# Sums of squares of MLA's queries taken while the queries arrive, and one root for all tokens; MLA's key roots for two token tiles at a time

## The chip, the cores and the metric

The kernel runs on one core of a Trainium2 chip. The time is that of one execution on the device, in microseconds (us). The engines are TensorE (PE; its weight loads are PEld), VectorE (DVE), ScalarE (ACT), GpSimd (POOL) and SyncE (SP), which only issues DMAs here.

## What is computed

One layer of a decoder for 1024 prompt tokens and 32 sample tokens (8 sequences of 4): a SwiGLU block, a mixer with two groups of heads side by side (a gated delta rule, GDN, and multi-head latent attention, MLA), and a second SwiGLU block. The change lies in the mixer's input, where one projection gives GDN's and MLA's raw values. MLA's part of the reference, cut to the norms that matter:

```python
def rms_norm(x, g):
    y = x * lax.rsqrt(jnp.mean(x * x, axis=-1, keepdims=True) + NORM_EPS)
    return y * g
...
    q = q_raw.reshape(B, T, 8, 64 + 32)                  # 8 heads of 96 columns
    qn = rms_norm(q[..., :64], qn_g)
    qr = apply_rope(rms_norm(q[..., 64:], qr_g), cos, sin)
    c = rms_norm(ckv_raw, ckv_g)                          # 128 wide
...
    kn = rms_norm(jnp.einsum('tr,rhd->thd', c, w_uk), kn_g)   # 8 heads of 64
```

So each token has 16 roots for its queries (per head one over 64 columns and one over 32) and 8 for its keys.

## The kernel before

All 1056 tokens go through together, as four blocks of 264 for the projections and as nine tiles for token-wise work: eight of 128 prompt tokens, and one (index 8) of the 32 sample tokens. Products of fp32 values are made from three matmuls of high and low halves (`mm3`, lines 127 to 129).

`mixer_in` is the stage of the change. Its order of work is the string `ORDER = "k0 k1 m0 m1 k2 k3 c0 I0 m2 m3 q0 m4 m5 z0 F0 q1 z1 q2 v0 q3 z2 v1 v2 v3 z3"`. Letters with weights (k, q, v, z for GDN, m for MLA's queries, c for its latent) are projections of 128 columns: `proj` loads the weights, splits them into halves `whi` (ScalarE) and `wlo` (GpSimd, four pieces, line 101; the first two sets on VectorE), multiplies the four token blocks (24 matmuls into a bank `pp` each), and after each block calls `hook`, which moves every generator in `self.active` on to its next `yield`. The first three sets (`bakr`, which holds the gates and the rotary key, then k0 and k1) go together, block by block. What follows a projection is such a generator:

- `mla_q_post` (m0 to m5): the 128 query columns are turned to tokens by TensorE (`to_tokens`, bank `ptk`, line 725), up to four tiles a bank; `sink` copies them to `mqt` (ScalarE, L1167), and two DMAs store them in DRAM (`qr_d`).
- `mla_q_finish` (F0, once all six are done, one tile after the other): a DMA loads the 768 columns of one tile (`mq`); a square (`mqs`, ScalarE, L1183), two reductions (VectorE, L1186), two scalings (L1187) and a root `hs` of ten VectorE instructions (`rsqrt`: L731, then three Newton steps of L737, L738, L739) follow; then the multiplications by the root (L1191, VectorE), by the gain (GpSimd, four pieces) and the rotation (`rope`, `rp`, VectorE and GpSimd by turns), and a DMA stores `qc_d`.
- `mla_c_post` (c0): the latent, its norm and transposed halves `cTh` and `cTl`, the rotary key, and then for each tile the key product `pkn`, its square `knq` (ScalarE, L1247), sum `kns` (VectorE, L1251), root `knr` (`pow_rs`, L760, and `rsqrt`), the value product `pv` and its copy `vtok` (ScalarE), and `kcat`, the scaled keys (VectorE L1263, GpSimd pieces, a GpSimd copy), stored in `kc_d`; values go to `v_d`.
- GDN's k, q and v: a convolution `cy` of four taps (ScalarE, then VectorE L938 three times), a SiLU back into `raw` (L940, L941), `to_tokens`, a sum of squares by the same scheme (`tsq` L954, one buffer; `tss` L955; root `trs`), the scaled `tok` (L963), transposes back (`pch`, L978) and products of pairs (`pk`, `dml`). `invert` (I0) solves triangular systems on VectorE (`inv`, `M`, lines 1107 and 1109).

Most tiles of the stage are the ten equal slots of tag `r` in the pool `tw`; PSUM has four banks of tag A (projections) and four of tag B (all else). `pieces(n, ...)` is n GpSimd instructions. The previous stage's last normalised input `nt` is read by `halve` (L372, L373).

The order on each engine is found by the framework's planner when the program is built: it plays the program through with a cost model of its own and gives each engine what is ready, first by the written order. GpSimd is exempt in this stage (`MW = ("Pool",)`): it keeps the written order, and its queue is strictly in turn. A tile that takes the place of an older one waits until that one is released.

Of the kernel before, what the change touches and what calls it, by code (L numbers as in the profile page):

```python
# [31 lines left out]
H = 8  # L32
# [52 lines left out]
class Kernel:  # L85
# [1075 lines left out]
    def mla_q_post(self, m, row, tp, ps):  # L1161
        nc = self.nc
        yield
        tok = self.r(tp, [P, NTL, P], "mqt")

        def sink(t0, n, sz, pt):
            nc.scalar.copy(tok[:sz, t0:t0 + n, :], pt[:sz, 0:n, :])  # L1167
        self.to_tokens(row, P, ps, sink)
        nc.sync.dma_start(out=self.qr_d[0:8, :, m * P:(m + 1) * P].rearrange("t p c -> p t c"), in_=tok[:, 0:8])
        nc.sync.dma_start(out=self.qr_d[8, :NS, m * P:(m + 1) * P], in_=tok[:NS, 8])  # L1170
        self.done["m"] += 1

    def mla_q_finish(self, t, rp, tp):

        nc = self.nc
        sz = P if t < 8 else NS
        q = self.r(rp, [P, 1, H, 96], "mq")
        if sz < P:
            nc.vector.memset(q, 0.0)
        qf = q.rearrange("p t h d -> p (t h d)")  # L1180
        nc.sync.dma_start(out=qf[:sz], in_=self.qr_d[t, :sz])
        sq = self.r(rp, [P, H, 96], "mqs")
        nc.scalar.activation(sq, q[:, 0], AF.Square)  # L1183
        ss = tp.tile([P, 3, 2, H], F32, tag="hs2", name="hs2", bufs=2)
        for n, (d0, d1) in enumerate(((0, 64), (64, 96))):
            nc.vector.tensor_reduce(out=ss[:, 0, n], in_=sq[:, :, d0:d1], axis=AX.X, op=ALU.add)  # L1186
            nc.vector.tensor_scalar(ss[:, 0, n], ss[:, 0, n], 1.0 / (d1 - d0), EPS, ALU.mult, ALU.add)  # L1187
        yield
        self.rsqrt(*(ss[:, n].rearrange("p a h -> p (a h)") for n in (1, 0, 2)))
        for n, (d0, d1) in enumerate(((0, 64), (64, 96))):  # L1190
            nc.vector.tensor_tensor(out=q[:, 0, :, d0:d1], in0=q[:, 0, :, d0:d1], in1=ss[:, 1, n].unsqueeze(2).to_broadcast([P, H, d1 - d0]), op=ALU.mult)  # L1191
        self.pieces(4, q[:, 0], q[:, 0], self.g_q.unsqueeze(1).to_broadcast([P, H, 96]), ALU.mult)
        yield
        self.rope(q[:, :, :, 64:96], H, q[:, :, :, 64:96], tp, t)
        if sz == P:
            nc.sync.dma_start(out=self.qc_d[t], in_=qf)
        else:
            nc.gpsimd.tensor_copy(self.qs, q[:NS, 0])
        yield
# [6 lines left out]
    def mla_c_post(self, row, tp, mp, ps, rp):  # L1206
        nc, o = self.nc, self.o
        yield
        c = self.r(rp, [P, NTL, 1, P], "ctok")
        nc.vector.memset(c[:, 8], 0.0)  # L1210

        def sink(t0, n, sz, pt):
            nc.scalar.copy(c[:sz, t0:t0 + n, 0, :], pt[:sz, 0:n, :])
        self.to_tokens(row, P, ps, sink)
        yield
        self.head_norm(c, 1, P, self.g_ckv, tp)
        yield
        nc.sync.dma_start(out=o["new_ckv_prompt"][0, 0].rearrange("(t p) c -> p t c", p=P), in_=c[:, 0:8, 0, :])
        nc.sync.dma_start(out=o["new_ckv_sample"][0].rearrange("s q c -> (s q) c"), in_=c[:NS, 8, 0, :])
        nc.gpsimd.tensor_copy(self.cs, c[:NS, 8, 0, :])  # L1220
        yield
        self.cTh, self.cTl = (self.r(rp, [P, NT], nm, F32R) for nm in ("cTh", "cTl"))
        for t0, n, sz in ((0, 4, P), (4, 4, P), (8, 1, NS)):
            pt = ps.tile([P, 512], F32, tag="B", name="pct")
            for t in range(n):
                nc.tensor.transpose(pt[:, t * P:t * P + sz], c[:sz, t0 + t, 0, :], self.ident[:sz, :sz])
            w = (n - 1) * P + sz
            nc.scalar.copy(self.cTh[:, t0 * P:t0 * P + w], pt[:, :w])
            nc.vector.tensor_tensor(out=self.cTl[:, t0 * P:t0 * P + w], in0=pt[:, :w], in1=f(self.cTh[:, t0 * P:t0 * P + w]), op=ALU.subtract)
            if t0 == 8:  # L1230
                nc.scalar.copy(self.csT, pt[:, :NS])
        yield
        kr = self.tb[:, :, 16:48].unsqueeze(2)
        self.head_norm(kr, 1, 32, self.g_kr, tp)
        self.kr = mp.tile([P, NTL, 1, 32], F32, name="kr")
        self.rope(kr, 1, self.kr, tp)
        nc.sync.dma_start(out=o["new_krope_prompt"][0, 0].rearrange("(t p) c -> p t c", p=P), in_=self.kr[:, 0:8, 0, :])
        nc.sync.dma_start(out=o["new_krope_sample"][0].rearrange("s q c -> (s q) c"), in_=self.kr[:NS, 8, 0, :])
        nc.gpsimd.tensor_copy(self.krs, self.kr[:NS, 8, 0, :])
        yield  # L1240
        for t in range(NTL):
            yield
            sz = P if t < 8 else NS
            pk = ps.tile([P, 512], F32, tag="B", name="pkn")
            self.mm3(pk[:sz], self.cTh[:, t * P:t * P + sz], self.cTl[:, t * P:t * P + sz], self.wuk[0], self.wuk[1], True, True)
            sq = tp.tile([P, 512], F32, tag="knq", name="knq", bufs=1)
            nc.scalar.activation(sq[:sz], pk[:sz], AF.Square)  # L1247
            ss = tp.tile([P, H], F32, tag="kns", name="kns", bufs=2)
            if sz < P:
                nc.vector.memset(ss, 1.0)  # L1250
            nc.vector.tensor_reduce(out=ss[:sz], in_=sq[:sz].rearrange("p (h d) -> p h d", h=H), axis=AX.X, op=ALU.add)  # L1251
            rs = tp.tile([P, H], F32, tag="knr", name="knr", bufs=2)
            self.pow_rs(rs, ss, H, 1.0 / 64, tp)
            if sz < P:
                nc.gpsimd.tensor_copy(self.rsn, rs[:NS])
                continue
            pv = ps.tile([P, 512], F32, tag="B", name="pv")
            self.mm3(pv, self.cTh[:, t * P:t * P + sz], self.cTl[:, t * P:t * P + sz], self.wuv[0], self.wuv[1], True, True)
            v = tp.tile([P, 512], F32, tag="vtok", name="vtok", bufs=1)
            nc.scalar.copy(v, pv)  # L1260
            nc.sync.dma_start(out=self.v_d[t], in_=v)
            kc = self.r(rp, [P, H, 96], "kcat")
            nc.vector.tensor_tensor(out=kc[:, :, 0:64], in0=pk.rearrange("p (h d) -> p h d", h=H), in1=rs.unsqueeze(2).to_broadcast([P, H, 64]), op=ALU.mult)  # L1263
            self.pieces(2, kc[:, :, 0:64], kc[:, :, 0:64], self.g_kn.unsqueeze(1).to_broadcast([P, H, 64]), ALU.mult)
            nc.gpsimd.tensor_copy(kc[:, :, 64:96], self.kr[:, t, :, :].to_broadcast([P, H, 32]))
            nc.sync.dma_start(out=self.kc_d[t], in_=kc.rearrange("p h d -> p (h d)"))

    def proj_z(self, m, tp, ps):
        nc = self.nc
# [14 lines left out]
    def mixer_in(self):  # L1284
# [12 lines left out]
        with tc.tile_pool(reuse_waits="tile", name="pswa", bufs=4, space=PSUM) as pa, tc.tile_pool(reuse_waits="tile", name="pswb", bufs=4, space=PSUM) as pb, tc.tile_pool(reuse_waits="tile", name="mw", bufs=1) as mp, tc.tile_pool(reuse_waits="tile", name="tw", bufs=1) as tp:  # L1297
            ps = Banks(A=pa, B=pb)

            def start(t, ml):  # L1300
                m = int(t[1])
                if t[0] == "k":
                    self.conv(4 + m, tp, ps, lambda raw: self.gdn_k(m, raw, tp, ps))
                elif t[0] == "q":
                    self.conv(m, tp, ps, lambda raw: self.gdn_q(m, raw, tp, ps))
                elif t[0] == "v":
                    self.conv(8 + m, tp, ps, lambda raw: self.gdn_v(m, raw, tp, ps))
                elif t[0] == "c":
                    self.mla_c(ml, mp, ps, tp)
                elif t[0] == "m":  # L1310
                    self.mla_q(m, tp, ps)
                elif t[0] == "z":
                    self.proj_z(m, tp, ps)
                elif t[0] == "I":
                    self.active.append(self.once("k", 4, self.invert(ml, tp)))
                elif t[0] == "F":
                    self.active.append(self.once("m", 6, self.in_turn([self.mla_q_finish(t, tp, ml) for t in range(NTL)])))
            with tc.tile_pool(reuse_waits="tile", name="tw0", bufs=1) as t0:
                row = self.r(tp, [P, NT], "bakr")
                self.proj(self.to_row(row), ps)  # L1320
# [9 lines left out]
            with tc.tile_pool(reuse_waits="tile", name="ml", bufs=1) as ml:  # L1330
                self.wuk = self.split_small(self.i["mla_w_uk"][0].rearrange("r h d -> r (h d)"), "wuk", lambda s, nm: self.r(tp, s, nm), self.keep)
                self.wuv = self.split_small(self.i["mla_w_uv"][0].rearrange("r h d -> r (h d)"), "wuv", lambda s, nm: self.r(tp, s, nm), ml)
                for t in order:
# [11 lines left out]
                    elif t[0] == "z":  # L1345
                        self.proj_z(m, tp, ps)
                    elif t[0] == "I":
                        self.active.append(self.once("k", 4, self.invert(ml, tp)))
                    elif t[0] == "F":
                        self.active.append(self.once("m", 6, self.in_turn([self.mla_q_finish(t, tp, ml) for t in range(NTL)])))  # L1350
                nc.vector.tensor_copy(self.eglK[0:64, 0:16, :], self.eglS[0:64].rearrange("p t c q -> p (t c) q"))
                nc.vector.tensor_copy(self.eglK[64:P, 1:17, :], self.eglS[64:P].rearrange("p t c q -> p (t c) q"))
                while self.active:
# [955 lines left out]
```

## Time and profile before

| | |
|---|---|
| three runs, median (lowest, highest) | 2799.54 us (2795.57, 2801.47) |
| the profiled execution | 2797.95 us |
| its span, first to last instruction | 2796.2 us |
| mean granted TensorE clock | 0.963 |
| VectorE, ScalarE, GpSimd busy | 60%, 39%, 39% of the span |

The page cuts the span into 40 equal slices of 69.9 us; the mixer's input lies in slices 12 to 18 of them. A row of a table by stretch gives the stretch, its length, each engine's busy time with the number of instructions in brackets, the granted clock as a share of full speed, and DMA figures. A row of waits reads "who waited, on what, <- who released it: total us, times, longest". A row of a timeline reads "start, duration, engine, line, operation, output <- input, shape, count, [idle before <- what ended it]". A group's row gives "busy us, mean ns | idle before it".

### The profile page before, as it was taken

What the parts mean: (1) busy time and instruction counts of PE and PEld (TensorE: products, weight loads), DVE (VectorE), ACT (ScalarE), POOL (GpSimd) and SP (SyncE); (2) the same over time, 40 slices, a digit from 0 to 9 for tenths busy, and PEclk for the clock granted to TensorE, in tenths of its full rate; (3) what the DMA queues carried; (4) which work ended last, traced back from release to release, by engine and by line L of the source; (5) the groups of instructions that cost most, each with busy time, mean ns of one, the idle gap of its engine ahead of it and who ended that gap; (6) DMA issues with size and microseconds to landing.
All of it is one profiled execution on the core that took longest, in us unless ns stands there. A gap on an engine that the chain in (4) does not pass through costs nothing.

```text
span 2796.2 us, 53185 instructions
## 1 busy us (share of the span) xinstructions
PE 2653.7 (95%) x21536; PEld 2453.3 (88%) x21536; DVE 1672.6 (60%) x3308; ACT 1077.5 (39%) x2060; POOL 1076.7 (39%) x1031
## 2 busy tenths in 40 slices
PE   5999999999999898799999999998989999999999
PEld 3789989999998888797888777776989999999999
DVE  7644444455564669866666566876485445445555
ACT  5322222322144533334666664553453333332111
POOL 0222222333342544643444464672433333333331
PEclk7999999999999899898999998997999999999999
DMA  7544442253232473433122243322522222225322
GB/s 277 180 142 148 133 144 88 71 191 100 82 99 79 138 194 122 157 111 115 45 51 64 60 89 110 97 74 68 178 85 84 80 78 77 84 77 187 99 78 70
DMA packets 339489, 308.33 MB, mean 110 GB/s; under 512 B 93866, under 2 KB 282018, under 8 KB 336172
## 3 DMA queue, kind: packets, MB, share of 16 engines
q1 hardware_dynamic: 304837, 246.32, 28.9%
q10 hardware_dynamic: 28262, 37.64, 4.2%
q0 software_dynamic: 6144, 20.98, 2.3%
q8 instruction: 169, 2.77, 0.4%
q14 instruction: 77, 0.62, 0.1%
HBM read 229.29 MB, written 75.59 MB: 109 GB/s over the span
## 4 chain that ended last, share of the span: by engine, by line
PE 74%; DVE 11%; DMA 5%; issue 4%; POOL 4%; ACT 2%; SPq 0%; ACTq 0%; POOLq 0%; DVEq 0%
PE po L129 7%; PE po L127 7%; PE po L128 7%; PE pY L127 4%; PE pY L128 4%; PE pY L129 4%; PE pX L127 3%; PE pX L128 3%; PE pX L129 3%; PE pZ L127 3%; PE pZ L128 3%; PE pZ L129 3%; PE kraw L127 2%; PE pp L127 2%; PE pp L128 2%
## 5 line engine op out<-in xcount | busy, mean ns | idle before, releaser
L129 PE MATMUL po<-act,wlo 128*128 128x264 f32 x1408 | 401.8, 285 | 0.0
L128 PE MATMUL po<-act,whi 128*128 128x264 f32 x1408 | 400.8, 285 | 1.0 <-DVE act L373 0.9
L127 PE MATMUL po<-act,whi 128*128 128x264 f32 x1408 | 400.5, 285 | 1.3 <-DVE x L444 0.7
L444 DVE SCALAR_TENSOR_TENSOR x<-po,modT,x 128x264 f32<-128x264 f32 (+1 forms) x416 | 195.3, 480 | 251.2 <-PE po L129 246.1
L127 PEld LDWEIGHTS po<-act,whi 128*128 128x128 f32 x1408 | 265.2, 188 | 2.1 <-DVE x L444 1.2
L128 PEld LDWEIGHTS po<-act,whi 128*128 128x128 f32 x1408 | 264.4, 188 | 1.4 <-DVE act L373 1.4
L129 PEld LDWEIGHTS po<-act,wlo 128*128 128x128 f32 x1408 | 264.7, 188 | 0.0
L373 POOL TENSOR_TENSOR A<-wg,A 128x512 fp32r<-128x512 f32 x84 | 113.9, 1356 | 357.4 <-ACT A L372 311.0
L2044 DVE TENSOR_REDUCE kss<-ksq 128x8 f32<-128x512 f32 x256 | 173.5, 681 | 101.7 <-ACT ksq L2043 100.0
L127 PE MATMUL pp<-hhi,whi 128*128 128x264 f32 (+1 forms) x768 | 225.5, 294 | 4.6 <-DVE nt L357 3.6
L128 PE MATMUL pp<-hlo,whi 128*128 128x264 f32 (+1 forms) x768 | 225.9, 294 | 0.0
L129 PE MATMUL pp<-hhi,wlo 128*128 128x264 f32 (+1 forms) x768 | 223.5, 291 | 0.0
L111 POOL TENSOR_TENSOR wlo<-wraw,whi 128x1024 fp32r<-128x1024 f32 x38 | 92.4, 2435 | 302.9 <-ACT whi L108 266.0
L127 PE MATMUL pX<-B,A 128*128 128x264 f32 x704 | 200.5, 289 | 7.8 <-ACT B L372 6.5
L128 PE MATMUL pX<-B,A 128*128 128x264 f32 x704 | 202.8, 288 | 4.9 <-DVE B L373 4.9
L2043 ACT ACTIVATE ksq<-kraw 128x512 f32<-128x512 f32 x256 | 152.7, 598 | 138.2 <-PE kraw L129 117.5
L127 PE MATMUL pY<-T,S 128*128 128x264 f32 x704 | 201.3, 286 | 2.8 <-DVE s L486 1.4
L128 PE MATMUL pY<-T,S 128*128 128x264 f32 x704 | 200.9, 285 | 2.1 <-DVE T L373 2.1
L129 PE MATMUL pX<-B,A 128*128 128x264 f32 x704 | 201.3, 286 | 0.0
L129 PE MATMUL pY<-T,S 128*128 128x264 f32 x704 | 199.9, 284 | 0.0
L1743 POOL TENSOR_TENSOR plo<-pf,phi 128x512 fp32r<-128x512 f32 (+1 forms) x96 | 96.7, 1013 | 191.9 <-ACT phi L1742 177.8
L486 DVE TENSOR_TENSOR cc<-u,pY 128x264 f32<-128x264 f32 x86 | 36.6, 426 | 205.8 <-PE pY L129 205.8
(555 smaller groups left out, 8217.4 us busy)
## 6 DMA issues: line engine op xcount, KB each, us to landing
adaw<-ada_w SPq DMA_DIRECT2D x72, 512.0 KB
wraw<-ffn_wi SPq DMA_DIRECT2D x46, 512.0 KB
act_d<-cc SPq DMA_DIRECT2D x88, 264.0 KB
wraw<-ffn_wo SPq DMA_DIRECT2D x44, 512.0 KB
wg<-ffn_wi SPq DMA_DIRECT2D x42, 512.0 KB
araw<-act_d ACTq DMA_DIRECT2D x160, 132.0 KB
x_d<-x SPq DMA_DIRECT2D x12, 1056.0 KB
wraw<-w_in SPq DMA_DIRECT2D x23, 512.0 KB
```

What stands on the lines that cost most here:

```text
L111: eng.tensor_tensor(out=lo, in0=raw, in1=f(hi), op=ALU.subtract)
L127: nc.tensor.matmul(out, whi, ahi, start=first, stop=False, **kw)
L128: nc.tensor.matmul(out, whi, alo, start=False, stop=False, **kw)
L129: return nc.tensor.matmul(out, wlo, ahi, start=False, stop=last, **kw)
L373: eng.tensor_tensor(out=lo, in0=src, in1=f(hi), op=ALU.subtract)
L444: nc.vector.scalar_tensor_tensor(out=x[:, d, :n], in0=ps[:, :n], scalar=self.modT[:, m, d, 0:1], in1=x[:, d, :n], op0=ALU.mult, op1=ALU.add)
L486: tt = lambda out, a, b, op=ALU.add: nc.vector.tensor_tensor(out=out, in0=a, in1=b, op=op)
L1743: nc.gpsimd.tensor_tensor(out=lo[:, off:], in0=pf[:, off:], in1=f(hi[:, off:]), op=ALU.subtract)
L2043: nc.scalar.activation(sq, kr, AF.Square)
L2044: nc.vector.tensor_reduce(out=ss[:, (j * 4 + m) * H:(j * 4 + m + 1) * H], in_=sq.rearrange("p (h d) -> p h d", h=H), axis=AX.X, op=ALU.add)
```

## The change

Queries: `sink` now also squares the bank (ScalarE, into `tsq`, the tag that GDN's sums use) and sums the squares by 32 columns on VectorE into `qg`, which holds 24 sums for each of nine tiles and is set to 1 by GpSimd when the stage begins. `mla_q_roots`, ahead of the tiles of F0, adds two sums of 32 for each 64, scales both kinds and takes one root over all 144 values of a partition (`qrs`). `mla_q_finish` loses square, sums and root, and multiplies by its part of `qrs`. Keys: tiles are taken in pairs; both are multiplied, squared and summed, then one `pow_rs` serves 16 roots, then each tile gets its `kcat`; a tile's values come after its keys and after one more `yield`.

```diff
@@ mla_q_post
         def sink(t0, n, sz, pt):
             nc.scalar.copy(tok[:sz, t0:t0 + n, :], pt[:sz, 0:n, :])
+            sq = tp.tile([P, 4, P], F32, tag="tsq", name="tsq", bufs=1)
+            nc.scalar.activation(sq[:sz, 0:n, :], pt[:sz, 0:n, :], AF.Square)
+            nc.vector.tensor_reduce(out=self.qg[:sz, t0:t0 + n, 4 * m:4 * m + 4], in_=sq[:sz, 0:n].rearrange("p t (c d) -> p t c d", d=32), axis=AX.X, op=ALU.add)
...
+    def mla_q_roots(self, rp):
+        nc = self.nc
+        g = self.qg.rearrange("p t (h c) -> p t h c", c=3)
+        hv = self.r(rp, [P, 2, NTL, 2, H], "hv")
+        v, t = hv[:, 0], hv[:, 1]
+        nc.vector.tensor_tensor(out=v[:, :, 0, :], in0=g[:, :, :, 0], in1=g[:, :, :, 1], op=ALU.add)
+        nc.vector.tensor_scalar(v[:, :, 0, :], v[:, :, 0, :], 1.0 / 64, EPS, ALU.mult, ALU.add)
+        nc.vector.tensor_scalar(v[:, :, 1, :], g[:, :, :, 2], 1.0 / 32, EPS, ALU.mult, ALU.add)
+        self.rsqrt(*(x.rearrange("p t a h -> p (t a h)") for x in (self.qrs, v, t)))
+        yield
@@ mla_q_finish
-        sq = self.r(rp, [P, H, 96], "mqs")
-        nc.scalar.activation(sq, q[:, 0], AF.Square)
-        ss = tp.tile([P, 3, 2, H], F32, tag="hs2", name="hs2", bufs=2)
+        yield
         for n, (d0, d1) in enumerate(((0, 64), (64, 96))):
-            nc.vector.tensor_reduce(out=ss[:, 0, n], in_=sq[:, :, d0:d1], axis=AX.X, op=ALU.add)
-            nc.vector.tensor_scalar(ss[:, 0, n], ss[:, 0, n], 1.0 / (d1 - d0), EPS, ALU.mult, ALU.add)
-        yield
-        self.rsqrt(*(ss[:, n].rearrange("p a h -> p (a h)") for n in (1, 0, 2)))
-        for n, (d0, d1) in enumerate(((0, 64), (64, 96))):
-            nc.vector.tensor_tensor(..., in1=ss[:, 1, n].unsqueeze(2).to_broadcast([P, H, d1 - d0]), op=ALU.mult)
+            nc.vector.tensor_tensor(..., in1=self.qrs[:, t, n].unsqueeze(2).to_broadcast([P, H, d1 - d0]), op=ALU.mult)
@@ mla_c_post
-        for t in range(NTL):
+        for ts in ((0, 1), (2, 3), (4, 5), (6, 7), (8,)):
             yield
-            (one tile: pkn, square, sum, pow_rs over 8; pv, vtok, v_d; kcat, kc_d)
+            for n, t in enumerate(ts):
+                (pkn, square, sum into ss[:, n * H:n * H + H])
+            rs = tp.tile([P, 2 * H], F32, tag="knr", name="knr", bufs=2)
+            self.pow_rs(rs, ss, 2 * H, 1.0 / 64, tp)
+            for n, t in enumerate(ts):
+                (kcat, kc_d)
+                yield
+                (pv, vtok, v_d)
@@ mixer_in, before anything else is placed in tw
+            self.qg = tp.tile([P, NTL, 3 * H], F32, name="qg")
+            nc.gpsimd.memset(self.qg, 1.0)
+            self.qrs = tp.tile([P, NTL, 2, H], F32, name="qrs")
...
-    self.in_turn([self.mla_q_finish(t, tp, ml) for t in range(NTL)])
+    self.in_turn([self.mla_q_roots(tp)] + [self.mla_q_finish(t, tp, ml) for t in range(NTL)])
```

More of the change, by code (lines that the diff above doesn't have):

```diff
@@ L1181, in mla_q_finish @@
         nc.sync.dma_start(out=qf[:sz], in_=self.qr_d[t, :sz])
-        sq = self.r(rp, [P, H, 96], "mqs")
-        nc.scalar.activation(sq, q[:, 0], AF.Square)
-        ss = tp.tile([P, 3, 2, H], F32, tag="hs2", name="hs2", bufs=2)
+        yield
         for n, (d0, d1) in enumerate(((0, 64), (64, 96))):
-            nc.vector.tensor_reduce(out=ss[:, 0, n], in_=sq[:, :, d0:d1], axis=AX.X, op=ALU.add)
-            nc.vector.tensor_scalar(ss[:, 0, n], ss[:, 0, n], 1.0 / (d1 - d0), EPS, ALU.mult, ALU.add)
-        yield
-        self.rsqrt(*(ss[:, n].rearrange("p a h -> p (a h)") for n in (1, 0, 2)))
-        for n, (d0, d1) in enumerate(((0, 64), (64, 96))):
-            nc.vector.tensor_tensor(out=q[:, 0, :, d0:d1], in0=q[:, 0, :, d0:d1], in1=ss[:, 1, n].unsqueeze(2).to_broadcast([P, H, d1 - d0]), op=ALU.mult)
+            nc.vector.tensor_tensor(out=q[:, 0, :, d0:d1], in0=q[:, 0, :, d0:d1], in1=self.qrs[:, t, n].unsqueeze(2).to_broadcast([P, H, d1 - d0]), op=ALU.mult)
         self.pieces(4, q[:, 0], q[:, 0], self.g_q.unsqueeze(1).to_broadcast([P, H, 96]), ALU.mult)
@@ L1240, in mla_c_post @@
         yield
-        for t in range(NTL):
+        for ts in ((0, 1), (2, 3), (4, 5), (6, 7), (8,)):
             yield
[L1243 to L1249, printed above, removed]
-                nc.vector.memset(ss, 1.0)
[L1251 to L1255, printed above, removed]
-                continue
[L1257 to L1266, printed above, removed]
@@ new lines, in mla_c_post @@
+            ss = tp.tile([P, 2 * H], F32, tag="kns", name="kns", bufs=2)
+            if ts == (8,):
+                nc.vector.memset(ss, 1.0)
+            pk = {}
+            for n, t in enumerate(ts):
+                sz = P if t < 8 else NS
+                pk[t] = ps.tile([P, 512], F32, tag="B", name="pkn")
+                self.mm3(pk[t][:sz], self.cTh[:, t * P:t * P + sz], self.cTl[:, t * P:t * P + sz], self.wuk[0], self.wuk[1], True, True)
+                sq = tp.tile([P, 512], F32, tag="knq", name="knq", bufs=1)
+                nc.scalar.activation(sq[:sz], pk[t][:sz], AF.Square)
+                nc.vector.tensor_reduce(out=ss[:sz, n * H:n * H + H], in_=sq[:sz].rearrange("p (h d) -> p h d", h=H), axis=AX.X, op=ALU.add)
@@ new lines, in mla_c_post @@
+            rs = tp.tile([P, 2 * H], F32, tag="knr", name="knr", bufs=2)
+            self.pow_rs(rs, ss, 2 * H, 1.0 / 64, tp)
+            if ts == (8,):
+                nc.gpsimd.tensor_copy(self.rsn, rs[:NS, :H])
+                continue
+            for n, t in enumerate(ts):
+                kc = self.r(rp, [P, H, 96], "kcat")
+                nc.vector.tensor_tensor(out=kc[:, :, 0:64], in0=pk[t].rearrange("p (h d) -> p h d", h=H), in1=rs[:, n * H:n * H + H].unsqueeze(2).to_broadcast([P, H, 64]), op=ALU.mult)
+                self.pieces(2, kc[:, :, 0:64], kc[:, :, 0:64], self.g_kn.unsqueeze(1).to_broadcast([P, H, 64]), ALU.mult)
+                nc.gpsimd.tensor_copy(kc[:, :, 64:96], self.kr[:, t, :, :].to_broadcast([P, H, 32]))
+                nc.sync.dma_start(out=self.kc_d[t], in_=kc.rearrange("p h d -> p (h d)"))
+                yield
+                pv = ps.tile([P, 512], F32, tag="B", name="pv")
+                self.mm3(pv, self.cTh[:, t * P:t * P + P], self.cTl[:, t * P:t * P + P], self.wuv[0], self.wuv[1], True, True)
+                v = tp.tile([P, 512], F32, tag="vtok", name="vtok", bufs=1)
+                nc.scalar.copy(v, pv)
+                nc.sync.dma_start(out=self.v_d[t], in_=v)
@@ L1316, in start @@
                 elif t[0] == "F":
-                    self.active.append(self.once("m", 6, self.in_turn([self.mla_q_finish(t, tp, ml) for t in range(NTL)])))
+                    self.active.append(self.once("m", 6, self.in_turn([self.mla_q_roots(tp)] + [self.mla_q_finish(t, tp, ml) for t in range(NTL)])))
             with tc.tile_pool(reuse_waits="tile", name="tw0", bufs=1) as t0:
@@ L1349, in mixer_in @@
                     elif t[0] == "F":
-                        self.active.append(self.once("m", 6, self.in_turn([self.mla_q_finish(t, tp, ml) for t in range(NTL)])))
+                        self.active.append(self.once("m", 6, self.in_turn([self.mla_q_roots(tp)] + [self.mla_q_finish(t, tp, ml) for t in range(NTL)])))
                 nc.vector.tensor_copy(self.eglK[0:64, 0:16, :], self.eglS[0:64].rearrange("p t c q -> p (t c) q"))
```

## The prediction

> **What bounds the kernel now.** I read the page first, then busy time by stage, then who TensorE waited for inside the stage that changes (the mixer's input, 837 to 1262 us), then the timelines of single engines around the longest waits.
>
> ```profile
> PE 2653.7 (95%) x21536; PEld 2453.3 (88%) x21536; DVE 1672.6 (60%) x3308; ACT 1077.5 (39%) x2060; POOL 1076.7 (39%) x1031
> core 0: us, PE busy (x) PEld busy (x) DVE busy (x) ACT busy (x) POOL busy (x), PEclk, DMA share, GB/s
> 1055.00:1072.00 17.00, 11.90 (x82) 10.52 (x81) 16.47 (x52) 6.45 (x14) 9.29 (x12) 0.92 0.29 98
> 1105.00:1130.00 25.00, 25.00 (x210) 24.99 (x209) 21.36 (x68) 9.68 (x19) 12.88 (x19) 1.00 0.27 91
> 1155.00:1180.00 25.00, 11.20 (x70) 10.47 (x69) 21.19 (x58) 6.36 (x12) 17.20 (x26) 0.70 0.32 113
> ...
> PE pch L978 <- DVE tok L963: 14.9, 3, 8.7
> PE ptk L725 <- DVE kcat L1263: 2.7, 2, 2.1
> ```
>
> Over the span TensorE is the bound (95%), so work taken from VectorE pays only where TensorE stands for it. It does here: in 1155 to 1180 us TensorE works 11.2 of 25 us while VectorE works 21.2, and the longest waits end on VectorE's `tok`. In 1105 to 1130 us, with VectorE as full, TensorE misses nothing.
>
> **The change, part by part.** *Queries.* Nine times over, two reductions, two scalings, a root of ten instructions and one 768-wide square go; 18 squares and 18 reductions come into the six sinks that turn query columns into tokens, and one root for all.
>
> ```profile
> L1186 DVE TENSOR_REDUCE hs<-mqs 128x8 f32<-128x512 f32 x9 | 6.1, 683 | 6.6 <-ACT mqs L1183 6.5
> L1186 DVE TENSOR_REDUCE hs<-mqs 128x8 f32<-128x256 f32 x9 | 3.7, 407 | 0.0
> L1187 DVE TENSOR_SCALAR hs<-hs 128x8 f32<-128x8 f32 x18 | 3.1, 204 | 0.0
> L731 DVE TENSOR_SCALAR hs<-hs 128x16 int32<-128x16 int32 x9 | 2.5, 280 | 0.0
> L737 DVE TENSOR_TENSOR hs<-hs 128x16 f32<-128x16 f32 x27 | 6.8, 254 | 0.3
> L738 DVE SCALAR_TENSOR_TENSOR hs<-hs 128x16 f32<-128x16 f32 x27 | 6.4, 240 | 0.4
> L739 DVE SCALAR_TENSOR_TENSOR hs<-hs 128x16 f32<-128x16 f32 x27 | 7.0, 261 | 0.3
> L955 DVE TENSOR_REDUCE tss<-tsq 128x8 f32<-128x512 f32 x16 | 10.9, 682 | 16.9 <-ACT tsq L954 16.8
> L955 DVE TENSOR_REDUCE tss<-tsq 32x2 f32<-32x128 f32 x8 | 2.1, 268 | 0.9 <-ACT tsq L954 0.9
> L1183 ACT ACTIVATE mqs<-mq 128x768 f32<-128x768 f32 x9 | 7.7, 850 | 7.9 <-DMA mq<-qr_d 7.9
> L954 ACT ACTIVATE tsq<-ptk 128x512 f32<-128x512 f32 x16 | 9.5, 597 | 13.3 <-DVE tss L955 9.9 <-PE ptk L725 3.2
> L737 DVE TENSOR_TENSOR pv<-rsk x16: 280/291/1279, 1316.5 to 1931.0; 128x128 f32<-128x128 f32 x16
> ```
>
> VectorE loses 6.1+3.7+3.1+2.5+6.8+6.4+7.0 = 35.6 us and gains 12 x 0.682 + 6 x 0.268 = 9.8 us in the sinks, and 13 root instructions over 72 or 144 values, taken at the 0.291 us of a 128-value step: 3.8 us. Net -22.0 us. ScalarE: -7.7 + 18 x 0.597 at most (six squares are of 32 rows and one tile) = +3.0 us at most, at nothing, since it works 6 to 10 us in each 25 shown; without that cover, 3.0. DMAs keep their number; the query loads no longer have a square behind them. The sinks run with their projections, m0 and m1 early, m2 to m5 beside the keys. The roots wait for the sixth sink's reduction; behind them stand only the nine scalings of `mq` and what GpSimd does with them. TensorE ran 25 of 25 us in projections from 1105, when these scalings were already due, so 3.8 us there cost nothing; were that cover gone, 3.8.
>
> *Keys.* Five root chains of eleven instead of nine; squares, sums, products and weights stay.
>
> ```profile
> L760 DVE TENSOR_SCALAR pv<-kns 128x8 f32<-128x8 f32 x9 | 2.2, 245 | 0.0
> L731 DVE TENSOR_SCALAR knr<-pv 128x8 int32<-128x8 int32 x9 | 1.7, 190 | 0.1
> L737 DVE TENSOR_TENSOR pv<-knr 128x8 f32<-128x8 f32 x27 | 5.4, 208 | 0.2
> L738 DVE SCALAR_TENSOR_TENSOR pv<-pv 128x8 f32<-128x8 f32 x27 | 6.8, 259 | 0.1
> L739 DVE SCALAR_TENSOR_TENSOR knr<-pv,knr 128x8 f32<-128x8 f32 x27 | 6.0, 231 | 0.2
> ```
>
> 22.1 us for 99, so 44 fewer are -9.8 us; four of the six sinks fall into the same stretch and add 4 x (2 x 0.682 + 0.268) = 6.5 us. Net -3.3 us of VectorE. Against it, two key banks instead of one are held until the joint root, in a pool of four that the transposes share (the 2.7 us of `ptk` behind `kcat` above), and a second square waits for the first sum. Values move behind the keys, their stores behind those of the keys on SyncE's queue. I take -2 us on the path: from -9 (that 2.7, and the 14.9 - 8.7 = 6.2 us that `tok` costs beside its longest wait, all gone) to +5 (twice the 2.7).
>
> *Where the queries' gain lands.* The two waits of 1155 to 1180 us:
>
> ```profile
> 1161.29 1.97 PE L725 MATMUL ptk<-ident,raw 128*128 128x128 f32 x8 [5.14 <-ACT raw L940]
> 1177.82 1.94 PE L978 MATMUL pch<-ident,tok 128*128 128x128 f32 x8 [8.66 <-DVE tok L963]
> ...
> 1144.05 0.66 DVE L731 TENSOR_SCALAR hs<-hs 128x16 int32<-128x16 int32 x1
> 1149.05 0.17 DVE L739 SCALAR_TENSOR_TENSOR hs<-hs 128x16 f32<-128x16 f32 x1
> 1155.93 4.16 DVE L938 SCALAR_TENSOR_TENSOR cy<-raw,convw,cy 128x1080 f32<-128x1080 f32 x2
> 1160.01 1.00 DVE L1186 TENSOR_REDUCE hs<-mqs 128x8 f32<-128x512 f32 x2
> 1167.34 0.17 DVE L739 SCALAR_TENSOR_TENSOR hs<-hs 128x16 f32<-128x16 f32 x1
> 1168.50 0.68 DVE L955 TENSOR_REDUCE tss<-tsq 128x8 f32<-128x512 f32 x1
> ...
> 1169.27 0.60 ACT L954 ACTIVATE tsq<-ptk 128x512 f32<-128x512 f32 x1 [5.75 <-DVE tss L955]
> ```
>
> Two query roots stand ahead of the work that TensorE lacks: 1144.05 to 1149.2 before the convolution (5.2 us), 1160.0 to 1167.5 before the sum that frees ScalarE's second square (5.75 us of waiting). Gone, they would bring the transposes 5.2 and then up to 5.75 us earlier: 11 of 13.8 us; with all 13.8 gone, the 11.2 us of work at clock 0.70 would also shrink by 3.4. What is late next is GpSimd, busy 17.2 of these 25 us, whose products the rope steps and `pch` need. So I take 9 us, from 4 (half of one wait taken over by GpSimd) to 17 (13.8 + 3.4).
>
> *A wait that is added.* `qg` is the first tile of the pool `tw`, and its memset the first GpSimd instruction of a stage in which GpSimd keeps the written order. The pool's first tile before was `bakr`:
>
> ```profile
> 839.09 8.34 POOL L101 TENSOR_TENSOR wlo<-wraw,whi 128x256 fp32r<-128x256 f32 x8 [10.38 <-ACT whi L676]
> ...
> 864.47 0.37 ACT L715 COPY bakr<-pp 48x264 f32<-48x264 f32 x1 [1.57 <-DVE zero L787]
> ...
> 861.96 2.43 DVE L373 TENSOR_TENSOR hlo<-nt,hhi 128x1056 fp32r<-128x1056 f32 x2 [3.00 <-ACT hhi L372]
> ...
> 865.40:880.20 14.80, 14.72 (x122) 14.51 (x120) 0.00 (x0) 2.76 (x9) 1.00 0.09 18
> ```
>
> `bakr`'s copy stood until VectorE had read `nt` for the last time (864.4): the pool seems to lie on the previous stage's `nt`. If the memset (216 values a partition; I put it under the 8.34 / 8 = 1.04 us of one product) waits for that too, the low halves of the weights of k1 and m0, queued behind it, go from 839 to about 865. Five projection blocks take 14.7 us (122 matmuls), 2.9 each; seven of the first twelve run before 865 now. If the scheduler puts other blocks ahead, six can still run before 865 (`bakr` and k0 on three of the four token blocks; the fourth is only halved at 864), and one block is late: +3 us (2.9 and a part of the split). If TensorE keeps the order, only the first two can, and five blocks are late: +15. If the tile lies elsewhere, 0. I take +3, as the planner orders TensorE by what is ready.
>
> *A rule against it.* VectorE stood 11.12 us in one subtraction while GpSimd ran 16 products without a pause:
>
> ```profile
> 1072.07 11.12 DVE L1109 TENSOR_TENSOR M<-M,inv 128x480 f32<-128x480 f32 x1
> 1072.05 2.35 POOL L101 TENSOR_TENSOR cy<-tok,egc 128x256 f32<-128x256 f32 x4
> 1074.37 8.31 POOL L101 TENSOR_TENSOR wlo<-wraw,whi 128x256 fp32r<-128x256 f32 x12
> ```
>
> A root step with two inputs can meet such a run. Quiet, the new roots cost 3.8 us, as taken; met once, 3.8 + 11 = 15, of which the range carries what exceeds the projections beside them. The Trainium skill, "SBUF — State Buffer", section "Who interferes with whom", says that of a two-input VectorE instruction and a reading GpSimd instruction the later one is blocked until the other ends. By it the roots would cost at most one product, 0.67 us ((2.35 + 8.31) / 16), more for each of 13 steps, 12.5 in all, an estimate; the trace's 11.12 us outlasts 16 such instructions, so the row decides.
>
> *Sum.* +3 (start) - 2 (keys) - 9 (queries) = -8 us on the profiled execution's 2797.95 us (span 2796.2): 2790. The median of the runs is 2799.54, 1.6 above that execution, so I forecast 2791.5.
>
> **Rivals.** *Slower: GpSimd's queue.* The memset waits and TensorE's order stays: +15. With 4 from the queries and nothing from the keys that is +11, 2810; it decides from the point where the start costs more than the 11 us gained later. For it: `bakr`'s wait, and GpSimd's written order. Against: nothing fixes TensorE's order there. *No change: the waits pass to another engine.* GpSimd's 17.2 of 25 us keep `tok` and `cy` where they are, and 4 from the queries meets 3 at the start: -1, 2798.5. For it: it is the busiest after VectorE there; against: many of its products are of `mq`, and come later only because VectorE's do. *Slower or equal: the sinks.* Query sinks were ScalarE alone; now the bank is free only after a square whose single buffer `tsq` waits for VectorE. If each of the four late sinks stands once as `tsq` did at 1169 (5.75 us), that is up to 23 us, less the 11 gained (queries and keys, the start at 0): +12, 2811; half of them, 2800. For it: VectorE works 16.5 of 17 us from 1055; against: the sums are short and only the second square waits.
>
> **How the numbers follow.** A measurement of this kernel tells about 0.2%, 5.6 us, from no change. Forecast, a gain over that: 0.5. Waits pass on: 0.2. GpSimd's queue: 0.17. Sinks: 0.13, of which 0.08 equal. So faster 0.5, same 0.28, slower 0.22. The forecast's own range is 2780 to 2794. All lower bounds together are 0 - 9 - 17 = -26, 2773.5; the upper cases end at 2811. I leave about 1 in 10 out on either side: 2777 to 2808.
>
> **What would show it.** Right: no `hs` steps, TensorE over 17 of 25 us in the stretch of `q1` and `z1` (now 1155 to 1180), waits for `tok` under 8 us (now 14.9), and the first new memset ending near 865 with one block late. Wrong: a TensorE wait over 5 us before 870 on `wlo`; `mqt` or `tsq` waiting for VectorE with `ptk` behind; a long step of `qrs` under a run of GpSimd products.

## The result, and the profile after

The changed kernel took 2782.56 us (median of four runs, 2780.05 to 2783.04) against 2798.95 for the kernel before in the same session (2795.57 to 2801.47): ratio 0.9945, 95% interval 0.9932 to 0.9958, or 15.4 us faster by the ratio. The forecast was 8 us. The profiled executions compared below took 2783.04 us (span 2781.2) and 2797.95 (span 2796.2).

The page's first row, and the stretches of the prediction (start:end, length, busy time of each engine with its instructions, granted clock, DMA):

```profile
PE 2650.7 (95%) x21536; PEld 2450.4 (88%) x21536; DVE 1646.6 (59%) x3169; ACT 1077.8 (39%) x2069; POOL 1084.4 (39%) x1032
...
1055.00:1072.00 17.00, 13.32 (x81) 11.86 (x80) 12.93 (x37) 7.12 (x16) 9.68 (x14) 0.80 0.56 194
1105.00:1130.00 25.00, 21.91 (x159) 21.40 (x157) 23.13 (x44) 7.35 (x18) 17.26 (x23) 0.86 0.31 97
1155.00:1180.00 25.00, 21.43 (x182) 20.37 (x182) 17.61 (x34) 9.65 (x21) 20.07 (x30) 0.98 0.57 190
```

VectorE has 139 instructions and 26.0 us fewer. By the prediction's terms 31.8 were due: 22.0 for the queries and 9.8 for the key roots (its net 3.3 for the keys sets 6.5 us of sinks against the 9.8, and those are in the 22.0 already). Among what grew are the scalings of `mq`, 14.6 us (L1199) in place of 10.0 (L1191). In 1155 to 1180 us TensorE now works 21.4 us at a clock of 0.98 (11.2 at 0.70 before), but in 1105 to 1130 us it works 21.9, where it worked all 25 before: part of the waiting came earlier. What it waited for in two stretches, first the kernel before, then the changed one (total, times, longest):

```profile
PE pch L978 <- DVE tok L963: 5.0, 1, 5.0
PE ptk L725 <- DVE dml L991: 3.7, 1, 3.7
PE ptk L725 <- DVE kcat L1263: 2.7, 2, 2.1
PE pv L127 <- DVE kcat L1263: 1.0, 1, 1.0
PE pv L127 <- ACT vtok L1260: 0.9, 1, 0.9
...
PE pch L978 <- DVE tok L963: 9.9, 2, 8.7
PE ptk L725 <- ACT raw L940: 5.1, 1, 5.1
PE pch L978 <- POOL cy L101: 3.3, 2, 2.3
...
```

```profile
PE pch L978 <- DVE tok L963: 2.0, 1, 2.0
PE pch L978 <- DVE kcat L1269: 1.4, 1, 1.4
PE ptk L725 <- DVE kcat L1269: 0.8, 1, 0.8
...
PE ptk L725 <- ACT raw L940: 12.3, 4, 5.2
PE pqg L1814 <- DVE qg L1810: 5.0, 1, 5.0
PE pch L978 <- DVE tok L963: 0.7, 1, 0.7
...
```

The first rows of each are 1010 to 1090 us (keys): 13.3 us of waits before, 5.2 after (lines left out are 0.7 us or less). The second are 1090 us to the end of the stage (queries): 18.9 before, and 3.7 more in its last wait, for `qg` (this `qg` is a tile of the attention, not the new one); 19.1 after, the `qg` row included. So by waits the keys' stretch gave 8 us and the queries' stretch 3.5: the waits for `tok` went there (9.9 to 0.7), those for `raw` grew from one of 5.1 to four of 12.3 together.

Four instants make an account of the whole: the first projection (837.27 before, 836.72 after), the copy of the latent, the first `pqg` (the attention's first product) and the end of the span.

```profile
975.03 1.21 ACT L715 COPY ckr<-pp 128x264 f32<-128x264 f32 x4
1262.49 0.56 PE L1798 MATMUL pqg<-ident,qg 32*96 32x32 f32 x8 [3.67 <-DVE qg L1794]
1266.69 1.91 PE L1648 MATMUL pqk<-ident,mtok 128*96 128x128 f32 x8 [2.65 <-DMA mtok<-qc_d]
```

```profile
975.69 1.21 ACT L715 COPY ckr<-pp 128x264 f32<-128x264 f32 x4
1251.19 0.85 PE L1814 MATMUL pqg<-ident,qg 32*96 32x32 f32 x8 [5.01 <-DVE qg L1810]
1254.48 1.92 PE L1664 MATMUL pqk<-ident,mtok 128*96 128x128 f32 x8 [0.60 <-DMA mtok<-qc_d]
```

Up to the first projection -0.6; from there to the latent +1.2 (the start); from the latent to `pqg` -12.0; behind it -3.7, of which 2.05 is the load of the queries (`qc_d`), which the attention now waits 0.60 us for; what is left of the 3.7 is less than executions differ there by chance (see below). Sum -15.0.

### The profile page after: what moved, and what is told of

It is laid out like the page before. It is cut to its first block, busy times and chain, and to the rows that moved or that the text cites. A ratio compares the mean times of both kernels' runs of the same rounds, so it can differ in the third digit from the quotient of the medians.

```text
span 2781.2 us, 53050 instructions
## 1 busy us (share of the span) xinstructions
PE 2650.7 (95%) x21536; PEld 2450.4 (88%) x21536; DVE 1646.6 (59%) x3169; ACT 1077.8 (39%) x2069; POOL 1084.4 (39%) x1032
## 4 chain that ended last, share of the span: by engine, by line
PE 75%; DVE 10%; DMA 5%; POOL 4%; issue 4%; ACT 2%; SPq 1%; ACTq 0%; DVEq 0%; POOLq 0%
PE po L127 7%; PE po L129 7%; PE po L128 6%; PE pY L127 4%; PE pY L128 4%; PE pY L129 4%; PE pX L127 3%; PE pX L128 3%; PE pX L129 3%; PE pZ L127 3%; PE pZ L128 3%; PE pZ L129 3%; PE kraw L127 2%; PE kraw L129 2%; PE kraw L128 2%
```

## The experiments

For each kernel the table gives the ratio to the kernel before, timed in the same session, and four instants of its profiled execution, counted from its own copy of the latent and set against the same of the kernel before: the start of the last piece of the SiLU (ScalarE L941) of q0, q1 and q2, and the first `pqg`. Minus is earlier. In the kernel before they are 82.46, 143.79, 186.12 and 287.46 us behind the latent.

| kernel | q0 | q1 | q2 | pqg | ratio [95%] |
|---|---|---|---|---|---|
| changed | -10.8 | -6.9 | -10.4 | -12.0 | 0.9945 [0.9932, 0.9958] |
| e1 queries alone | -0.2 | +0.6 | -5.1 | -7.2 | 0.9986 [0.9975, 0.9997] |
| e2 keys alone | -10.8 | -7.0 | -4.1 | +0.1 | 0.9989 [0.9979, 0.9998] |
| e3 memset on VectorE | -11.1 | -4.0 | -9.7 | -12.2 | 0.9951 [0.9936, 0.9966] |
| e4 memset alone | -2.6 | -3.7 | -3.7 | -1.8 | 0.9985 [0.9971, 0.9998] |
| e5 old roots beside | -11.9 | -3.0 | -5.3 | -0.7 | 1.0015 [1.0005, 1.0026] |
| e6 single key roots | -6.2 | -0.4 | -6.1 | -7.5 | 0.9959 [0.9947, 0.9971] |
| e7 keys tile by tile | -8.4 | +2.9 | -0.9 | -1.8 | 0.9984 [0.9973, 0.9995] |
| e8 F0 later | -11.9 | -9.6 | -13.6 | -13.8 | 0.9946 [0.9929, 0.9963] |
| e9 keys alone, F0 later | -11.5 | -11.6 | -7.9 | -3.4 | 0.9977 [0.9967, 0.9988] |
| e10 before, F0 later | -0.9 | -4.2 | +1.1 | +3.1 | 1.0015 [1.0005, 1.0025] |
| e11 key roots by threes | -7.9 | -9.9 | -16.5 | -20.2 | 0.9931 [0.9915, 0.9946] |
| e12 key roots by fours | +0.7 | -4.0 | -10.0 | -12.3 | 0.9961 [0.9946, 0.9976] |

The instants are of one execution each, and executions of one kernel lie up to 20 us apart over the whole span (e4: 2781.85 to 2801.63), so the ratio decides and the instants say where. Much of that spread lies behind the stage: from `pqg` to the end, where the program is the same in all, the fourteen profiled executions (the kernel before and the thirteen below) took 1520 to 1542 us. They also name a slip of mine: the waits of 1155 to 1180 us, which I had called those of q1 and z1, are q2's (186.12 + 975.03 = 1161.15).

**e1, the queries alone.** The loop over key tiles as in the kernel before:

```diff
-        for ts in ((0, 1), (2, 3), (4, 5), (6, 7), (8,)):
+        for t in range(NTL):        # and the old body
```

> The queries' part alone (sums of squares in the sinks, one root; keys tile by tile as before; the memset of qg at the start as in the changed kernel). The whole change gave -16.4 us. Theory 'queries' (the waits for VectorE between 1130 and 1251 us carry the gain): -9 to -13 us against before, with no hs steps, and most of the 11.2 us of TensorE work in 1155 to 1180 us raised above 17. Theory 'keys' (the freed VectorE time between 1011 and 1090 us is where it starts): -3 to -6. Rival 'replanning' (any edit here moves TensorE's order, and the gain belongs to no part): anything from +5 to -16, with the gain at places where neither part has steps.

Measured: -3.9 us by the ratio (-0.8 to -7.0). Gained from q2 on, as the queries' theory had it, but much less than forecast: the size is the one that the theory "keys" gave (-3 to -6). A wait of the sinks came in:

```profile
1089.05 2.13 PE L725 MATMUL ptk<-ident,mqr 128*128 128x128 f32 x8 [5.05 <-ACT tsq L1169]
```

That is the rival "sinks" in the size that it was priced at (5.75), once. In the changed kernel it isn't there. It hangs on the keys' order: the square waited 6.87 us for VectorE's sum into `qg`, which stood behind one subtraction of `M` (L1109) that took 11.12 us from 1073.80 on. The wait of 3.7 us for `dml` that stood behind `M` before is gone in its place, so the sinks cost 1.4 us net.

**e2, the keys alone.** The new loop over pairs, and the queries as before.

> The keys' part alone (roots for two tiles at a time, values behind the keys; queries with their squares, sums and roots per tile; no qg). Theory 'queries': -2 to -5 us, gained between 1011 and 1090 us, and the 13.8 us of waits in 1155 to 1180 us stay. Theory 'keys': -8 to -12, those waits fall too, since what comes before them is done earlier. Rival 'replanning': anything from +5 to -10.

Measured: -3.1 us (-0.6 to -5.9), as by the queries' theory in sum, and not in course: q0 and q1 come as early as in the changed kernel, and all of it is lost again by `pqg`. The root steps `hs` of two query tiles stand ahead of `tok`, seven of them and one scaling at 0.65 to 0.70 us each, and TensorE stands:

```profile
1159.84 0.65 DVE L738 SCALAR_TENSOR_TENSOR hs<-hs 128x16 f32<-128x16 f32 x1
1160.53 0.65 DVE L739 SCALAR_TENSOR_TENSOR hs<-hs 128x16 f32<-128x16 f32 x1
1170.75 1.42 DVE L963 TENSOR_TENSOR tok<-tok,trs 128x1024 f32<-128x1024 f32 x2
1172.12 1.09 PE L978 MATMUL pch<-ident,tok 128*128 128x128 f32 x4 [7.32 <-DVE tok L963]
```

So the parts aren't additive: 3.9 and 3.1 alone, 15.4 together. The ends of the intervals just meet (12.9 at most for the two alone, 11.8 at least together), so the size of the gap is loose.

**e5, the old query roots beside the new one.** In each `mla_q_finish`:

```diff
+        nc.scalar.activation(sq, q[:, 0], AF.Square)
+        (two sums, two scalings; after the yield the root of ten steps; the result goes nowhere)
         nc.vector.tensor_tensor(..., in1=self.qrs[:, t, n] ..., op=ALU.mult)
```

> The changed kernel, and beside it again per query tile the old square, two sums, two scalings and ten root steps, whose result nobody uses: 35.6 us of VectorE come back at their old places, and nobody waits for them but what stands behind them on VectorE. Theory 'what stands ahead on VectorE' (query roots ahead of the convolution and of tok between 1144 and 1178 us use up what the keys gain): like the keys alone; 10 us ahead of before near 1100 us, back to 0 to 2 ahead at the end of the stage, -2 to -5 in all against before, with a wait for tok of 5 us or more after 1150. Rival 'chain of a tile' (the multiplications of mq wait for their own square, sums and root): -10 to -15, as changed. Rival 'replanning': -5 with no such wait.

Measured: +4.2 us against before (+1.4 to +7.3), 19 to 20 slower than the changed kernel. Early at q0 (-11.9), nothing left at `pqg`, and the wait is back:

```profile
1160.54 0.65 DVE L738 SCALAR_TENSOR_TENSOR mqs<-mqs 128x16 f32<-128x16 f32 x1
1173.66 1.94 PE L978 MATMUL pch<-ident,tok 128*128 128x128 f32 x8 [7.35 <-DVE tok L963]
```

Nothing waits for the result of these steps; what they hold up is what stands behind them on VectorE, behind 9 squares on ScalarE, or on the slot of tag `r` that their tile takes (not told apart here). The rival "chain of a tile" falls; the loss is larger than either theory said. Part of it is plain: this kernel also keeps the sinks and the new roots, so its VectorE is busy for 1674.7 us, 11.9 more than with the keys alone (1662.8) and 2.1 more than before. In the profiled executions, counted from the span's start, `pqg` comes 12.0 us later than in the changed kernel; the rest of the loss lies behind the stage, where executions also differ by chance.

**e10 and e9, F0 one place later**, in the kernel before and with the keys alone. I meant to take the query roots out of the way of q0 and q1.

```diff
-ORDER = "... m4 m5 z0 F0 q1 z1 q2 ..."
+ORDER = "... m4 m5 z0 q1 F0 z1 q2 ..."
```

> The kernel before with F0 one place later and nothing else: what the move does by itself. Theory 'place': -4 to -8 us (the 5.1 and 8.7 us of waits in 1155 to 1180 shrink). Theory 'amount': within 3 us of before, with waits for tok that move to q1 and q2.

> The keys' part alone, as in the run of the keys alone, with F0 one place later in the written order (z0 q1 F0 z1), so that the nine query roots, kept whole, begin behind the first tok and cy of q0. With the keys alone the ten microseconds gained by 1100 were gone by 1160, and at 1157 to 1172 the root steps hs (0.65 us each) stood among those of tok. Theory 'place': moved away from there, the roots leave the keys' gain: -8 to -12 us against before. Theory 'amount' (VectorE has 35.6 us too much of work up to the end of the stage, wherever it stands): the wait moves to q1's or q2's tok, and the kernel stays at -2 to -5.

Measured: e10 +4.2 us (+1.4 to +7.0), e9 -6.4 (-3.4 to -9.2). With the wait to be relieved being q2's, the move put the roots onto it: it grew from 8.66 to 12.96 us in e10, and is 11.84 in e9.

```profile
1175.60 1.97 PE L978 MATMUL pch<-ident,tok 128*128 128x128 f32 x8 [12.96 <-DVE tok L963]
```

```profile
1167.73 1.97 PE L978 MATMUL pch<-ident,tok 128*128 128x128 f32 x8 [11.84 <-DVE tok L963]
```

"Place" as I had put it fails (e10 was to gain 4 to 8). "Amount" had the wait move to q2, as it did; e9's -6.4 lies between the two theories. What is left of "place": with the same place of F0 the keys are worth 10.6 us (0.9977 against 1.0015), more than the 3.1 with F0 where it was, so how much of a gain survives does depend on what stands where.

**e8, the changed kernel with F0 later.**

> The changed kernel with F0 one place later in the written order (z0 q1 F0 z1): the nine tiles' multiplications and rotations start about 25 us later. Theory 'what stands ahead on VectorE': the convolution of q0 and q1 no longer shares VectorE and GpSimd with them, so the waits for raw at 1112 and 1150 us (3.1 and 5.2) shrink: -3 to -6 against the changed kernel. Rival: the same 13 us of multiplications then meet q2 and v0, and the wait moves there: within 2 us; or the last qc_d comes too late for the attention's first load (waiting 0.6 us now), and it is 3 to 10 slower.

Measured: as the changed kernel (0.9946). The waits for `raw` shrank (3.06 to 2.43 and 5.20 to 0.82), q2 waits 6.05 us for `tok`, and the last wait for the attention's `qg` grew from 5.01 to 7.71: the rival, a wait that moves.

**e6 and e7, which part of the keys.** e6 keeps the pairs and takes a root for each tile; e7 takes the tiles one by one, with the values still behind the keys.

```diff
-            self.pow_rs(rs, ss, 2 * H, 1.0 / 64, tp)
+            for n in range(len(ts)):
+                self.pow_rs(rs[:, n * H:n * H + H], ss[:, n * H:n * H + H], H, 1.0 / 64, tp)
```

> The changed kernel with a root chain for each key tile again (nine of eleven steps in place of five; pairs of tiles, values behind the keys, all else kept). Theory 'root steps' (44 fewer steps, 9.8 us of VectorE, are the keys' gain): the keys' gain falls away, so like the queries alone, 4 to 7 us slower than the changed kernel, with the multiplications of kcat later. Rival 'order' (pairing and values behind the keys let TensorE go on with the transposes while the roots run): within 2 us of the changed kernel.

```diff
-        for ts in ((0, 1), (2, 3), (4, 5), (6, 7), (8,)):
+        for ts in [(t,) for t in range(NTL)]:
```

> The changed kernel with the keys tile by tile as in the kernel before (nine chains of eleven root steps), but each tile's values still behind its keys and one more yield. Theory 'root steps': 4 to 7 us slower than the changed kernel, as with the roots single. Rival 'order of the values' : within 2 us of the changed kernel. If it is slower here and not with single roots in pairs, the pairing of the products is what helps.

Measured: e6 -11.5 us against before (-8.1 to -14.8), 3.9 less than the changed kernel by the two ratios, whose intervals overlap; its q1 and `pqg` stand where the queries alone have them, as the theory "root steps" had it. The ratios say otherwise: e6 is 7.6 us ahead of the queries alone, and those two intervals don't overlap. e7 -4.5 (-1.4 to -7.6), 7.0 behind e6 with the same number of root steps, and those intervals don't overlap either. So the ratios give more of the keys' gain to the pairs and the instants of e6 give it to the merged roots; which of the two it is stays open. e7 tells less than I meant: it also has 17 yields where the pairs have 13, so the last `kcat` of its keys is scaled at 1092.42 us (1071.92 with pairs), in the queries' stretch.

**e3 and e4, the memset at the start.** e3 sets the new `qg` on VectorE; e4 is the kernel before plus `qg`, `qrs` and the memset on GpSimd, read by nobody.

```diff
-            nc.gpsimd.memset(self.qg, 1.0)
+            nc.vector.memset(self.qg, 1.0)
```

> The changed kernel with the memset of qg on VectorE in place of GpSimd. GpSimd then makes the low halves of the weights of k1 and m0 from 839 us, as before. If the start cost what the prediction took: -3 us against the changed kernel (2779.5). If GpSimd's standing pays for itself, because VectorE's last norm runs 3.4 us earlier beside an idle GpSimd (the last read of nt at 861.0 in place of 864.4): within 1 us of the changed kernel, with nt read last at 864 again. Rival 'replanning': differs from the changed kernel by 3 to 8 us, at places after 900.

> The kernel before with nothing added but the tiles qg and qrs at the head of the pool tw and qg's memset on GpSimd, which nobody reads. The wait at the start alone: +3 us by the prediction, +0.6 by the landmarks of the changed kernel's trace (last copy of bakr 875.72 against 875.19, latent's copy 975.69 against 975.03), +15 by the rival of GpSimd's queue. Rival 'replanning': a shift of more than 4 us of either sign that arises after 900 us, where this kernel does nothing else.

Measured: e3 as the changed kernel (0.9951), e4 -4.2 us (-0.6 to -8.1). From the first projection to the last copy of `bakr` it takes 37.6 to 38.2 us in the kernels whose GpSimd starts on the weights at 838 to 839 (before, e2, e3, e9, e10), and 39.0 in those where it waits (changed, e1, e4, e6, e7, e8, e11, e12; 40.5 in e5): the wait costs 1 us. It costs no more because VectorE, alone, is done sooner. e3, then e4:

```profile
838.77 8.34 POOL L101 TENSOR_TENSOR wlo<-wraw,whi 128x256 fp32r<-128x256 f32 x8 [10.35 <-ACT whi L676]
861.63 2.43 DVE L373 TENSOR_TENSOR hlo<-nt,hhi 128x1056 fp32r<-128x1056 f32 x2 [3.00 <-ACT hhi L372]
```

```profile
857.86 2.42 DVE L373 TENSOR_TENSOR hlo<-nt,hhi 128x1056 fp32r<-128x1056 f32 x2 [3.00 <-ACT hhi L372]
860.34 0.28 POOL L1301 MEMSET qg<- 128x216 f32 x1 [32.81 <-DVE zero L787]
```

From the first projection (836.95 and 836.07) the last read of `nt` begins 24.7 us later in e3 and 21.8 in e4. That e4 gains 4.2 at all is not explained by its only instruction. I take it for what planning the program anew moved (-2.6 to -3.7 at q0 to q2); no run shows that. e1's -3.9 and e2's -3.1 by the ratio are no more than this gain of a kernel that does no less work, so the argument about the parts rests on the instants of 7 to 11 us and on ratios of 10 us and more.

**e11 and e12, larger groups.** Three chains in place of five, by groups of tiles (8, 0, 1), (2, 3, 4), (5, 6, 7) and (0, 1, 2, 3), (4, 5, 6, 7), (8).

> The changed kernel with key roots for three token tiles at a time (three chains over 24 values, the sample tokens with the first pair, in place of five chains). 22 root steps fewer. Theory 'root steps': -2 to -5 us against the changed kernel. Rival 'banks': three of the four banks of tag B are held until the joint root, the transposes of m3 and q0 wait for kcat 3 to 6 us more, and the kernel is 3 to 8 us slower than the changed one.

> Key roots for four token tiles at a time and one chain for the sample tokens: three chains as with three tiles at a time, but all four banks of tag B are held until the joint root. Theory 'root steps' (the number of chains sets the gain): as with three tiles, 0.993 of before within the interval. Rival 'banks' (TensorE's transposes, which use the same four banks, stand while all are held): waits of 3 us or more for kcat between 1010 and 1070 us, and 5 to 10 us slower than with three tiles.

Measured: threes 2775.36 us, -19.3 against before (-15.1 to -23.8), the fastest of all; the interval overlaps with the changed kernel's by 0.14%, and the two were not timed in one session. Fours: -10.9, 8.4 behind threes with the same number of root steps. In fours TensorE waits for a bank:

```profile
1049.88 0.79 PE L127 MATMUL pv<-wuvh,cTh 128*128 128x512 f32 x1 [4.75 <-DVE kcat L1270]
```

So "root steps" was not contradicted up to three banks, and "banks" came in with four. In threes TensorE waited 0.8 us for `kcat` in the keys' stretch (2.2 in the changed kernel), and 6.0 for GpSimd's `cy`.

## Why the prediction was right, and where it was wrong

*Sum and sign* were right, the size half of what came (-8 against -15.4), inside the range. That the sum came that near is partly luck: the parts alone gave 3.1 (keys) and 3.9 (queries) where 2 and 9 were forecast, and some 8 of the 15.4 came only with both, for which the sum had no term.

*Start, +3: about +1.* The memset waited for the last read of `nt` and TensorE was reordered, as said. Mis-sized was the lateness: I put it at one block from 864 to 865, and left out that an idle GpSimd lets VectorE read `nt` 2.9 us earlier.

```profile
861.01 0.28 POOL L1313 MEMSET qg<- 128x216 f32 x1 [32.81 <-DVE zero L787]
861.25 5.58 POOL L101 TENSOR_TENSOR wlo<-wraw,whi 128x256 fp32r<-128x256 f32 x8
```

*Keys, -2: near what they gave alone (3.1), too small beside the queries.* By waits 8 us went in their stretch, near the -9 at the far end of the range: 3.7 for `dml`, 3.0 for `tok`, the rest for `kcat` and `vtok`. The step that failed: I weighed VectorE's net 3.3 us against banks, and took the 11.12 us for which `M` stood as a risk to the roots, not as something that the new order would move. The kernel before, then the changed one:

```profile
1071.53 0.55 POOL L1255 COPY rsn<-knr 32x8 f32<-32x8 f32 x1 [3.44 <-DVE knr L739]
1087.41 1.28 DVE L991 TENSOR_TENSOR dml<-pk,dml 128x512 f32<-128x512 f32 x2
1088.15 0.40 PE L725 MATMUL ptk<-ident,mqr 128*32 128x128 f32 x1 [3.68 <-DVE dml L991]
```

```profile
1062.69 2.37 POOL L101 TENSOR_TENSOR cy<-tok,egc 128x256 f32<-128x256 f32 x4 [5.39 <-DVE tok L963]
1078.98 0.67 DVE L991 TENSOR_TENSOR dml<-pk,dml 128x512 f32<-128x512 f32 x1
1085.46 0.58 POOL L1265 COPY rsn<-knr 32x8 f32<-32x8 f32 x1 [10.19 <-DVE knr L739]
1086.02 5.58 POOL L101 TENSOR_TENSOR wlo<-wraw,whi 128x256 fp32r<-128x256 f32 x8
1086.04 6.11 DVE L1109 TENSOR_TENSOR M<-M,inv 128x512 f32<-128x512 f32 x1
```

Before, GpSimd's queue stood at `rsn` until the last key root was done, and then ran the products of `cy` and two sets of `wlo` without a pause; `M` stood through them, `dml` behind `M`, and TensorE 3.68 us for `dml`. Now `cy` runs earlier, the run behind `rsn` is shorter, `M` stands 6.11 us, and `dml` is done before it. In e12 `M` stands 5.56 us ahead of `dml`, and TensorE waits 3.44 for `dml` again; in e4 and e10, where the keys are the old ones, `M` stands 11.12 and 11.13 as before. The banks that I had feared cost little with two tiles (`kcat` 3.7 us of waits before, 2.2 after).

*Queries, -9: right only together with the keys.* Of the two waits, `tok`'s 8.66 went and `raw`'s stayed:

```profile
1140.80 2.92 DVE L1199 TENSOR_TENSOR mq<-mq,qrs 128x512 f32<-128x512 f32 x2 [1.98 <-DMA mq<-qr_d]
1143.64 5.85 DVE L938 SCALAR_TENSOR_TENSOR cy<-raw,convw,cy 128x1080 f32<-128x1080 f32 x3
1150.69 1.97 PE L725 MATMUL ptk<-ident,raw 128*128 128x128 f32 x8 [5.20 <-ACT raw L940]
```

The `hs` steps ahead of the convolution are gone, but it now stands behind a pair of scalings of `mq` that takes 2.92 us (1.02 at 1102.84) while GpSimd multiplies, and waits 5.20 against 5.14. Three more waits for `raw` came in (3.06, 2.72 and 1.38). That is the rival "the waits pass to GpSimd" for one wait of the two, as the trace has it; no run tested it alone. The step that failed is the form of the sum: I added keys and queries. Alone, the queries gained 3.9; given the keys, 12.3 (15.4 - 3.1). The keys bring TensorE early to a stretch that VectorE bounds (e2, e5), and the queries take the bound away.

*Sinks:* not in the changed kernel; 5.05 us in e1, behind `M`. *New roots:* thirteen steps of 0.19 to 0.31 us between 1094.95 and 1102.4, beside projections and with GpSimd idle (it waited 12.40 us for the first `mq`), as said.

*What would show it:* no `hs` steps, TensorE over 17 of 25 us (21.4) and waits for `tok` under 8 (2.7 from 1010 us on) came. The 21.4 flatters, since the work of q2 now comes 9.7 us earlier: in the 25 us that lie as the old stretch did to q2 (1145.3 to 1170.3) it is 18.95 at a clock of 0.86, still over 17. Of the late block only about 1 us of 2.9 came, and the memset ended at 861.3, not near 865.

## What to carry to other kernels

Two cuts of one engine's work in neighbouring stretches need not be worth the sum of what each gives alone: here they were worth more together, since what TensorE gained in the first stretch was lost again while VectorE bounded the next (e2, e5). So look at the stretch behind before pricing one. An instruction in an in-order queue that waits for a late result (`rsn` here) gathers work behind it that then runs in one block; see what stands beside that block. When small roots are merged over tiles, count the banks that are held until the joint root: with two and three of the four banks the kernel was faster than before, with all four TensorE waited 4.75 us for one and part of the gain was gone. Whether the merged roots or the pairs pay isn't settled here.

## What the hardware showed beside that

In the eleven kernels with `M` held 6 us or more (all but e7, e11 and e12), `M` began 0.02 to 0.03 us after a run of GpSimd's products and ended about 0.5 us after it (its usual length is 0.65 to 0.70): 11.12 us with sixteen products, 6.11 with eight. With threes, VectorE was not held inside such a run; GpSimd ran 12 products from 1073.03 to 1083.73, and the two-input steps that began in its middle took about their usual 0.67, up to 1.1:

```profile
1077.38 1.07 DVE L1107 TENSOR_TENSOR inv<-M 128x510 f32<-128x510 f32 x1
1078.97 0.67 DVE L1109 TENSOR_TENSOR M<-M,inv 128x510 f32<-128x510 f32 x1
...
1073.03 10.70 POOL L101 TENSOR_TENSOR wlo<-wraw,whi 128x256 fp32r<-128x256 f32 x12
```

So what was held began with the run or near it (0.5 us behind in e12, 5.56 us), but not all that began so was held: in the kernel before, eight products ran from 839.09 to 847.4 without a pause, and a two-input step that began at 839.18 took 0.70 us. Why, stays open, and no run aimed at it. The Trainium skill, "SBUF — State Buffer", section "Who interferes with whom", has the later of two such instructions blocked for the whole of the other one. That fits the 1.1 us of a step within a run; it doesn't give 6 or 11 us, which outlast eight and sixteen GpSimd instructions.
